# A sliding-window matmul: wider column groups, longer rows per load, fewer and larger weight loads

## The chip, the cores and the metric

The kernel runs on one core of a Trainium2 chip. The core has a matrix engine (TensorE, PE in the profile, with PEld for its weight loads), VectorE (DVE), ScalarE (ACT), GpSimd (POOL) and SyncE (SP). They share an on-chip memory (SBUF, 128 partitions), TensorE writes its sums to a second one (PSUM), and 16 DMA engines move data between SBUF and the external memory (HBM). A DMA is issued by an instruction on SP, ACT or POOL; of these only POOL's DMAs change the data type under way ("casting"). The metric is the device time in microseconds (us) of one execution. One MiB below is 1,048,576 bytes, and sizes of loads are given on their fp32 side, where they are read.

## The reference: what is computed

```python
B, S, D, W = 4, 4096, 4096, 64        # x (B,S,D), w (D,D) fp32, offsets (B,) int64
for b in range(B):
    o = int(offsets[b])
    results.append(x[b, o:o+W] @ w)
return np.stack(results)
```

Four windows of 64 rows, each at an offset known only at run time, are multiplied by the same 4096 x 4096 matrix w. Stacked, that is a 256 x 4096 matrix times w. The kernel reads 64 MiB of w and 4 MiB of x and writes 4 MiB.

## The kernel before

The windows are taken in two pairs (`G` = 2, index `g`); the two windows of a pair fill the 128 partitions of `xpair[g]`. The contraction over D runs in 32 k tiles of 128 rows of w. The output's columns are done in four groups `ng` of `NG` = 1024 columns, each in two halves of `NT` = 512 (index `j`).

Loads of w. The first three k tiles of group 0 come as plain fp32 DMAs from SP and ACT (L70) and are cast to fp16 by ACT (L79). Everything else of w comes as casting DMAs on POOL, one k tile of one group at a time: 128 rows of 1024 values, so 4 KB read per row and 0.5 MiB per load, into one of 36 buffers `wh`. Eight are issued at once (L74); the rest follow in the order of use (L112). The very last k tile of the last group is loaded in two halves (L107, `wlast`).

x. The offsets are loaded by SP to SBUF (L68), read into POOL registers (L83), and used as addresses by four casting DMAs on POOL (L94), each 64 rows of 4096 values, 16 KB read per row and 1 MiB per load. They stand in POOL's order behind the eight loads of L74 and ahead of those of L112.

Transposes. TensorE multiplies each 128 x 128 block of `xpair[g]` with an identity (L125), which leaves the transposed block in PSUM, and VectorE copies eight blocks at a time as fp16 into `xT[g]` (L132).

Main loop. For each group, for each k tile, for g and j, TensorE runs one matmul of 128 x 512 (L146). PSUM is four tiles of 1024 columns; odd and even groups use different pairs of them, so that one group's results can be copied out (ACT L159/L164, VectorE L160/L165) while the next group runs. Group 0 is stored by SP and ACT at once (L161, L162). Groups 1 and 2 are stored by POOL (L167). The last group is finished half by half (L175), copied out (L187, L188) and stored by SP and ACT (L192 to L196).

Order. Tile, the framework, places the waits between engines and schedules instructions; each engine then works through its own list in order. On POOL, every load of w stands ahead of the stores of L167. POOL's DMAs use eight completion semaphores in turn, so each DMA from the ninth on waits until the one eight places earlier has landed; a load also waits until its buffer's last reader is done.

Of the kernel before, what the change touches and what calls it, by code (L numbers as in the profile page):

```python
# [9 lines left out]
@with_exitstack  # L10
def kernel(
    ctx: ExitStack,
    tc: tile.TileContext,
    x: bass.AP,
    w: bass.AP,
    offsets: bass.AP,
    out: bass.AP,
):
    nc = tc.nc
    fp32 = mybir.dt.float32  # L20
    fp16 = mybir.dt.float16

    B, S, D = x.shape
    _, N = w.shape
    WIN = out.shape[1]
    P = 128
    KT = 128
    NT = 512
    NG = 1024
    n_k = D // KT  # L30
    n_ng = N // NG
    n_sub = NG // NT
    G = B // 2

    POOL = mybir.EngineType.Pool

    const_pool = ctx.enter_context(tc.tile_pool(name="const", bufs=1))
    x_pool = ctx.enter_context(tc.tile_pool(name="xp", bufs=1))
    wh_pool = ctx.enter_context(tc.tile_pool(name="wh", bufs=36))
    w32_pool = ctx.enter_context(tc.tile_pool(name="w32", bufs=1))  # L40
    whh_pool = ctx.enter_context(tc.tile_pool(name="whh", bufs=2))
    st_pool = ctx.enter_context(tc.tile_pool(name="st", bufs=1))
    sth_pool = ctx.enter_context(tc.tile_pool(name="sth", bufs=4))
    psum_pool = ctx.enter_context(tc.tile_pool(name="ps", bufs=1, space=bass.MemoryType.PSUM))

    identity = const_pool.tile([P, P], fp16, name="identity")
    off_t = const_pool.tile([1, B], mybir.dt.int64, name="off_t")

    xpair = [x_pool.tile([P, D], fp16, name=f"xpair{g}") for g in range(G)]
    xT = [x_pool.tile([P, D], fp16, name=f"xT{g}") for g in range(G)]  # L50

    ps = [psum_pool.tile([P, NG], fp32, name=f"ps{t}") for t in range(4)]

    wh_tiles = {}

    def w_tile(ng, ki):
        t = wh_pool.tile([P, NG], fp16, name="wh", tag="wh")
        wh_tiles[(ng, ki)] = t
        return t

    def w_src(ng, ki):
        return w[ki * KT : (ki + 1) * KT, ng * NG : (ng + 1) * NG]

    N_EARLY = 3
    early_q = [nc.sync, nc.scalar, nc.sync]
    w32 = [w32_pool.tile([P, NG], fp32, name=f"w32_{k}") for k in range(N_EARLY)]

    nc.sync.dma_start(out=off_t[:], in_=offsets[None, :])  # L68
    for k in range(N_EARLY):
        early_q[k].dma_start(out=w32[k][:], in_=w_src(0, k))  # L70

    n_pre = 8
    for ki in range(N_EARLY, N_EARLY + n_pre):
        nc.gpsimd.dma_start(out=w_tile(0, ki)[:], in_=w_src(0, ki))  # L74

    make_identity(nc, identity[:])

    for k in range(N_EARLY):
        nc.scalar.copy(out=w_tile(0, k)[:], in_=w32[k][:])  # L79

    off_i32 = off_t.bitcast(mybir.dt.int32)
    off_vals = [
        nc.values_load(  # L83
            off_i32[0:1, 2 * b : 2 * b + 1],
            engines=[POOL],
            min_val=0,
            max_val=S - WIN,
        )
        for b in range(B)
    ]  # L90

    for b in range(B):
        g, m = divmod(b, 2)
        nc.gpsimd.dma_start(  # L94
            out=xpair[g][m * WIN : (m + 1) * WIN, :],
            in_=x[b][bass.ds(off_vals[b], WIN), :],
        )

    wlast = [
        whh_pool.tile([P, NT], fp16, name="whl", tag="whl") for _ in range(n_sub)  # L100
    ]
    for ng in range(n_ng):
        for ki in range(N_EARLY + n_pre if ng == 0 else 0, n_k):
            if ng == n_ng - 1 and ki == n_k - 1:
                for j in range(n_sub):
                    cs = ng * NG + j * NT
                    nc.gpsimd.dma_start(  # L107
                        out=wlast[j][:],
                        in_=w[ki * KT : (ki + 1) * KT, cs : cs + NT],
                    )  # L110
            else:
                nc.gpsimd.dma_start(out=w_tile(ng, ki)[:], in_=w_src(ng, ki))  # L112

    stage = {}
    for ng in (1, 2):
        for g in range(G):
            stage[(ng, g)] = st_pool.tile(
                [P, NG], fp32, name=f"stage{ng}{g}", tag=f"stage{ng}{g}"
            )

    for g in range(G):
        for t in range(4):
            for q in range(8):
                k = 8 * t + q
                nc.tensor.matmul(  # L125
                    out=ps[t][:, q * KT : (q + 1) * KT],
                    lhsT=xpair[g][:, k * KT : (k + 1) * KT],
                    rhs=identity[:],
                    start=True,
                    stop=True,  # L130
                )
            nc.vector.tensor_copy(  # L132
                out=xT[g][:, t * NG : (t + 1) * NG], in_=ps[t][:]
            )

    for ng in range(n_ng):
        par = ng % 2
        acc = [ps[2 * par], ps[2 * par + 1]]
        last = ng == n_ng - 1
        cs = ng * NG  # L140
        n_full = n_k - 1 if last else n_k
        for ki in range(n_full):
            whk = wh_tiles[(ng, ki)]
            for g in range(G):
                for j in range(n_sub):
                    nc.tensor.matmul(  # L146
                        out=acc[g][:, j * NT : (j + 1) * NT],
                        lhsT=xT[g][:, ki * KT : (ki + 1) * KT],
                        rhs=whk[:, j * NT : (j + 1) * NT],
                        start=(ki == 0),  # L150
                        stop=(ki == n_k - 1),
                    )
        if not last:
            if ng == 0:
                st0 = [
                    st_pool.tile([P, NG], fp32, name=f"stage0{g}", tag="stage0")
                    for g in range(G)
                ]
                nc.scalar.copy(out=st0[0][:], in_=acc[0][:])  # L159
                nc.vector.tensor_copy(out=st0[1][:], in_=acc[1][:])  # L160
                nc.sync.dma_start(out=out[0:2, :, cs : cs + NG], in_=st0[0][:])  # L161
                nc.scalar.dma_start(out=out[2:4, :, cs : cs + NG], in_=st0[1][:])  # L162
            else:
                nc.scalar.copy(out=stage[(ng, 0)][:], in_=acc[0][:])  # L164
                nc.vector.tensor_copy(out=stage[(ng, 1)][:], in_=acc[1][:])  # L165
                for g in range(G):
                    nc.gpsimd.dma_start(  # L167
                        out=out[2 * g : 2 * g + 2, :, cs : cs + NG],
                        in_=stage[(ng, g)][:],
                    )  # L170
        else:
            ki = n_k - 1
            for j in range(n_sub):
                for g in range(G):
                    nc.tensor.matmul(  # L175
                        out=acc[g][:, j * NT : (j + 1) * NT],
                        lhsT=xT[g][:, ki * KT : (ki + 1) * KT],
                        rhs=wlast[j][:],
                        start=False,
                        stop=True,  # L180
                    )
                hs = cs + j * NT
                sth = [
                    sth_pool.tile([P, NT], fp32, name="sth", tag="sth")
                    for _ in range(G)
                ]
                nc.scalar.copy(out=sth[0][:], in_=acc[0][:, j * NT : (j + 1) * NT])  # L187
                nc.vector.tensor_copy(  # L188
                    out=sth[1][:], in_=acc[1][:, j * NT : (j + 1) * NT]
                )  # L190
                if j == 0:
                    nc.sync.dma_start(out=out[0:2, :, hs : hs + NT], in_=sth[0][:])  # L192
                    nc.sync.dma_start(out=out[2:4, :, hs : hs + NT], in_=sth[1][:])
                else:
                    nc.scalar.dma_start(out=out[0:2, :, hs : hs + NT], in_=sth[0][:])
                    nc.sync.dma_start(out=out[2:4, :, hs : hs + NT], in_=sth[1][:])  # L196


# [28 lines left out]
```

## Time and profile before

| what | value |
|---|---|
| median of 10 runs | 188.76 us (188.65 to 189.15) |
| profiled execution | 188.69 us |
| its span | 187.0 us |
| mean granted TensorE clock | 0.987 |
| PE busy | 132.0 us (71%) in 576 matmuls |
| VectorE, ScalarE, POOL busy | 14.3, 8.5, 71.9 us |
| HBM read, written | 71.30 MB, 4.19 MB: 404 GB/s over the span |
| POOL's DMA queue | 19040 packets, 36.97 MB |
| a load of w by L112, from issue to landing | 9.5 us (median) |
| first x load issued, last x load landed | 9.26 us, 28.38 us |
| first main matmul | 31.80 us |

The span runs from the first to the last record of the profiled execution; its own time is 1.7 us longer. "Busy" of a DMA engine is the time that packets took. GB/s and MB of the DMA rows count the bytes written, so a casting load shows half of what it reads. In the DMA packets of POOL's queue, each row of a load or store is one packet, and each DMA adds 16 small ones, which report that it is complete.

### The profile page before, as it was taken

To read this page: it belongs to the slowest core of one execution; us is meant where nothing else is said; L and a number is where in the kernel's file an instruction comes from. 1 tells how busy PE (TensorE), PEld (TensorE's weight loads), DVE (VectorE), ACT (ScalarE), POOL (GpSimd) and SP (SyncE) were. 2 spreads that over 40 slices of the span, in tenths; PEclk is the share of its full clock that TensorE was granted. 3 is DMA by queue.
4 is the path that set the end of the run, shared out by engine and by line. 5 is a ranking of instruction groups with operands and counts; after the bars stand their busy time and mean duration, and the time that the engine had idled before them with its cause. 6 is when DMAs were issued, how large, how long until landed. Compare 5 with 4: busy or idle time off the path is not lost.

```text
span 187.0 us, 1496 instructions
## 1 busy us (share of the span) xinstructions
PE 132.0 (71%) x576; PEld 56.0 (30%) x576; DVE 14.3 (8%) x13; ACT 8.5 (5%) x9; POOL 71.9 (38%) x140
## 2 busy tenths in 40 slices
PE   0000079999999967688788888888888888788820
PEld 0000078444444422223332332332323323323300
DVE  0000079200000020000002000000020000000020
ACT  2410000000002000000002000000020000000020
POOL 7343124333343433344344434434443426344200
PEclk9999999999999999999999999999999999999995
DMA  5999999999999999999999999999999999999994
GB/s 148 291 203 219 217 203 209 210 209 209 210 209 209 248 225 241 230 209 209 210 209 209 209 209 209 210 209 209 211 209 209 210 209 209 209 210 209 254 415 164
DMA packets 20344, 40.72 MB, mean 218 GB/s; under 512 B 2290, under 2 KB 2546, under 8 KB 20082
## 3 DMA queue, kind: packets, MB, share of 16 engines
q0 software_dynamic: 19040, 36.97, 102.3%
q1 hardware_dynamic: 866, 2.36, 3.3%
q10 hardware_dynamic: 432, 1.31, 2.2%
q8 instruction: 4, 0.07, 0.1%
q14 instruction: 2, 0.02, 0.0%
HBM read 71.30 MB, written 4.19 MB: 404 GB/s over the span
## 4 chain that ended last, share of the span: by engine, by line
DMA 70%; PE 18%; issue 5%; POOL 2%; DVE 0%; ACT 0%; POOLq 0%
DMA wh<-in_w_dram 63%; PE ps L146 15%; DMA xpair<-in_x_dram 8%; PE ps L125 2%; POOL wh L112 1%; POOL wh L74 1%; PE ps L175 1%; DVE sth L188 0%; ACT sth L187 0%; POOLq L112 0%; POOLq L211 0%
## 5 line engine op out<-in xcount | busy, mean ns | idle before, releaser
L146 PE MATMUL ps<-wh,xT 128*128 128x512 f16 x508 | 123.9, 378 | 22.4 <-DMA wh<-in_w_dram 22.3
L112 POOL DMA_DIRECT2D wh<-in_w_dram x116 | 61.5, 531 | 92.3 <-DMA wh<-in_w_dram 74.6
L146 PEld LDWEIGHTS <-xT 128*128 128x128 f16 x508 | 49.0, 97 | 96.8 <-issue 45.9
L125 PE MATMUL ps<-identity,xpair 128*128 128x128 f16 x64 | 7.1, 310 | 24.7 <-DMA xpair<-in_x_dram 24.7
L125 PEld LDWEIGHTS <-xpair 128*128 128x128 f16 x64 | 6.7, 144 | 24.9 <-issue 24.9
L132 DVE CAST xT<-ps 128x1024 f16<-128x1024 f32 x8 | 9.2, 1218 | 24.7 <-PE ps L125 24.7
L165 DVE COPY stage<-ps 128x1024 f32<-128x1024 f32 x2 | 2.5, 1225 | 68.0 <-PE ps L146 68.0
L164 ACT COPY stage<-ps 128x1024 f32<-128x1024 f32 x2 | 2.0, 1012 | 77.4 <-PE ps L146 77.4
L74 POOL DMA_DIRECT2D wh<-in_w_dram x8 | 4.4, 585 | 0.8 <-POOLq L211 0.8
L188 DVE COPY sth<-ps 128x512 f32<-128x512 f32 x2 | 1.4, 692 | 38.5 <-PE ps L175 38.5
L94 POOL DMA_DIRECT2D xpair<-in_x_dram x4 | 2.1, 522 | 5.5 <-DMA wh<-in_w_dram 5.5
L160 DVE COPY stage<-ps 128x1024 f32<-128x1024 f32 x1 | 1.2, 1225 | 34.7 <-DMA out_dram<-stage 34.7
L167 POOL DMA_DIRECT2D out_dram<-stage x4 | 2.1, 534 | 3.1 <-DMA wh<-in_w_dram 3.1
L159 ACT COPY stage<-ps 128x1024 f32<-128x1024 f32 x1 | 1.0, 1013 | 49.0 <-PE ps L146 49.0
L79 ACT CAST wh<-w 128x1024 f16<-128x1024 f32 x3 | 3.0, 1042 | 4.6 <-DMA w<-in_w_dram 4.6
L187 ACT COPY sth<-ps 128x512 f32<-128x512 f32 x2 | 1.2, 586 | 38.9 <-PE ps L175 38.9
L175 PE MATMUL ps<-whl,xT 128*128 128x512 f16 x4 | 1.3, 378 | 0.5 <-ACT sth L187 0.5
L107 POOL DMA_DIRECT2D whl<-in_w_dram x2 | 1.1, 530 | 1.3 <-DMA wh<-in_w_dram 1.3
L79 ACT ACT_TABLE_LOAD x1 | 1.3, 1283 | 1.3 <-PEq L211 1.3
L175 PEld LDWEIGHTS <-xT 128*128 128x128 f16 x4 | 0.4, 97 | 1.1 <-issue 0.5
masks.py:199 POOL TENSOR_SCALAR_AFFINE_SELECT identity<-identity 128x128 f16<-128x128 f16 x1 | 0.3, 289 | 0.1
masks.py:197 POOL MEMSET identity<- 128x128 f16 x1 | 0.3, 290 | 0.0
(4 smaller groups left out, 0.4 us busy)
## 6 DMA issues: line engine op xcount, KB each, us to landing
wh<-in_w_dram POOLq DMA_DIRECT2D x124, 256.0 KB, 9.5
xpair<-in_x_dram POOLq DMA_DIRECT2D x4, 512.0 KB, 12.8
out_dram<-stage POOLq DMA_DIRECT2D x4, 512.0 KB, 8.3
w<-in_w_dram SPq DMA_DIRECT2D x2, 512.0 KB, 6.3
out_dram<-sth SPq DMA_DIRECT2D x3, 256.0 KB, 5.6
w<-in_w_dram ACTq DMA_DIRECT2D x1, 512.0 KB, 4.3
out_dram<-stage SPq DMA_DIRECT2D x1, 512.0 KB, 8.3
out_dram<-stage ACTq DMA_DIRECT2D x1, 512.0 KB, 7.0
```

Source lines behind the costliest of these rows:

```text
L74: nc.gpsimd.dma_start(out=w_tile(0, ki)[:], in_=w_src(0, ki))
L79: nc.scalar.copy(out=w_tile(0, k)[:], in_=w32[k][:])
L94: nc.gpsimd.dma_start(out=xpair[g][m * WIN : (m + 1) * WIN, :], in_=x[b][bass.ds(off_vals[b], WIN), :],)
L112: nc.gpsimd.dma_start(out=w_tile(ng, ki)[:], in_=w_src(ng, ki))
L125: nc.tensor.matmul(out=ps[t][:, q * KT : (q + 1) * KT], lhsT=xpair[g][:, k * KT : (k + 1) * KT], rhs=identity[:], start=True, stop=True,)
L132: nc.vector.tensor_copy(out=xT[g][:, t * NG : (t + 1) * NG], in_=ps[t][:])
L146: nc.tensor.matmul(out=acc[g][:, j * NT : (j + 1) * NT], lhsT=xT[g][:, ki * KT : (ki + 1) * KT], rhs=whk[:, j * NT : (j + 1) * NT], start= ...
L164: nc.scalar.copy(out=stage[(ng, 0)][:], in_=acc[0][:])
L165: nc.vector.tensor_copy(out=stage[(ng, 1)][:], in_=acc[1][:])
L167: nc.gpsimd.dma_start(out=out[2 * g : 2 * g + 2, :, cs : cs + NG], in_=stage[(ng, g)][:],)
L175: nc.tensor.matmul(out=acc[g][:, j * NT : (j + 1) * NT], lhsT=xT[g][:, ki * KT : (ki + 1) * KT], rhs=wlast[j][:], start=False, stop=True,)
L188: nc.vector.tensor_copy(out=sth[1][:], in_=acc[1][:, j * NT : (j + 1) * NT])
```

## The change

The column groups become two of 2048 columns, with four matmul tiles of 512 in each; PSUM is eight tiles of one bank, and both groups use the same eight. The first k tile of w is loaded for all 4096 columns at once by one plain fp32 DMA on ACT (128 rows of 16 KB, 2 MiB) and cast by ACT in two pieces. On POOL one casting load of k tile 1 (128 rows of 8 KB, 1 MiB) comes first, then the identity, then the four x loads, whose offsets are read from SBUF to a register one by one, right ahead of each load, without the bounds checks at run time. All further loads of w read 8 KB rows; most of them take two k tiles in one DMA (2 MiB), and the last four or five of each group one. There are 12 buffers, each large enough for two k tiles. The eviction of the transposes is split between VectorE and ACT in pieces of 512 columns. The order of instructions is that of the program text (`manual_schedule`). The first group is stored by POOL after all loads, the second by ACT and SP, 1 MiB per DMA.

```diff
-    KT = 128
     NT = 512
-    NG = 1024
-    n_k = D // KT
+    NG = 2048
+    n_k = D // P
...
-    wh_pool = ctx.enter_context(tc.tile_pool(name="wh", bufs=36))
+    wh_pool = ctx.enter_context(tc.tile_pool(name="wh", bufs=12))
...
+    ps = [psum_pool.tile([P, NT], fp32, name=f"bank{t}") for t in range(8)]
...
+    ctx.enter_context(tc.manual_schedule())
 
     nc.sync.dma_start(out=off_t[:], in_=offsets[None, :])
-    for k in range(N_EARLY):
-        early_q[k].dma_start(out=w32[k][:], in_=w_src(0, k))
+    nc.scalar.dma_start(out=w0_32[:], in_=w[0:P, :])
+    off_i32 = off_t.bitcast(mybir.dt.int32)
 
-    n_pre = 8
-    for ki in range(N_EARLY, N_EARLY + n_pre):
-        nc.gpsimd.dma_start(out=w_tile(0, ki)[:], in_=w_src(0, ki))
+    def load(ng, ki, n):
+        t = wh_pool.tile([P, n * NG], fp16, name="wh", tag="wh")
+        nc.gpsimd.dma_start(
+            out=t[:].rearrange("p (t n) -> p t n", t=n),
+            in_=w[ki * P : (ki + n) * P, ng * NG : (ng + 1) * NG].rearrange(
+                "(t p) n -> p t n", p=P
+            ),
+        )
+        for i in range(n):
+            wh[(ng, ki + i)] = t[:, i * NG : (i + 1) * NG]
 
+    wh = {(ng, 0): w0_16[:, ng * NG : (ng + 1) * NG] for ng in range(n_ng)}
+    load(0, 1, 1)
     make_identity(nc, identity[:])
-    for k in range(N_EARLY):
-        nc.scalar.copy(out=w_tile(0, k)[:], in_=w32[k][:])
...
+    for b in range(B):
+        g, m = divmod(b, 2)
+        o = nc.values_load(
             off_i32[0:1, 2 * b : 2 * b + 1],
             engines=[POOL],
             min_val=0,
             max_val=S - WIN,
+            skip_runtime_bounds_check_because="offsets are drawn below S - WIN",
         )
+        nc.gpsimd.dma_start(
+            out=x16[g][m * WIN : (m + 1) * WIN, :],
+            in_=x[b][bass.ds(o, WIN), :]
+        )
+    for ng in range(n_ng):
+        for ki in range(n_k):
+            if (ng, ki) not in wh:
+                load(ng, ki, 2 if ki < n_k - 4 - (ki % 2) else 1)
...
+    nc.scalar.copy(out=w0_16[:, :NG], in_=w0_32[:, :NG])
+    nc.scalar.copy(out=w0_16[:, NG:], in_=w0_32[:, NG:])
...
+            dst = xT[g][:, t * NT : (t + 1) * NT]
+            if t % 2 == 0:
+                nc.vector.tensor_copy(out=dst, in_=ps[t][:])
+            else:
+                nc.scalar.copy(out=dst, in_=ps[t][:])
...
+        for ki in range(n_k):
             for g in range(G):
                 for j in range(n_sub):
+                    mm(g, j, ki, wh[(ng, ki)][:, j * NT : (j + 1) * NT], ki == 0, ki == n_k - 1)
+        for j in range(n_sub):
+            for g in range(G):
+                dst = stage[ng][g][:, j * NT : (j + 1) * NT]
+                if g == 0:
+                    nc.scalar.copy(out=dst, in_=ps[4 * g + j][:])
                 else:
+                    nc.vector.tensor_copy(out=dst, in_=ps[4 * g + j][:])
+        for g in range(G):
+            (q[g] if last else nc.gpsimd).dma_start(
+                out=out[2 * g : 2 * g + 2, :, ng * NG : (ng + 1) * NG],
+                in_=stage[ng][g][:],
+            )
```

More of the change, by code (lines that the diff above doesn't have):

```diff
@@ L38 @@
     x_pool = ctx.enter_context(tc.tile_pool(name="xp", bufs=1))
-    wh_pool = ctx.enter_context(tc.tile_pool(name="wh", bufs=36))
-    w32_pool = ctx.enter_context(tc.tile_pool(name="w32", bufs=1))
-    whh_pool = ctx.enter_context(tc.tile_pool(name="whh", bufs=2))
+    wh_pool = ctx.enter_context(tc.tile_pool(name="wh", bufs=12))
     st_pool = ctx.enter_context(tc.tile_pool(name="st", bufs=1))
-    sth_pool = ctx.enter_context(tc.tile_pool(name="sth", bufs=4))
     psum_pool = ctx.enter_context(tc.tile_pool(name="ps", bufs=1, space=bass.MemoryType.PSUM))
@@ L47 @@
     off_t = const_pool.tile([1, B], mybir.dt.int64, name="off_t")
-    xpair = [x_pool.tile([P, D], fp16, name=f"xpair{g}") for g in range(G)]
+    w0_32 = x_pool.tile([P, N], fp32, name="w0row")
+    w0_16 = x_pool.tile([P, N], fp16, name="w0half")
+    x16 = [x_pool.tile([P, D], fp16, name=f"xrow{g}") for g in range(G)]
     xT = [x_pool.tile([P, D], fp16, name=f"xT{g}") for g in range(G)]
[L52 to L66, printed above, removed]
-    nc.sync.dma_start(out=off_t[:], in_=offsets[None, :])
-    for k in range(N_EARLY):
-        early_q[k].dma_start(out=w32[k][:], in_=w_src(0, k))
-    n_pre = 8
-    for ki in range(N_EARLY, N_EARLY + n_pre):
-        nc.gpsimd.dma_start(out=w_tile(0, ki)[:], in_=w_src(0, ki))
-    make_identity(nc, identity[:])
-    for k in range(N_EARLY):
-        nc.scalar.copy(out=w_tile(0, k)[:], in_=w32[k][:])
-    off_i32 = off_t.bitcast(mybir.dt.int32)
-    off_vals = [
-        nc.values_load(
+    ps = [psum_pool.tile([P, NT], fp32, name=f"bank{t}") for t in range(8)]
+    ctx.enter_context(tc.manual_schedule())
+    nc.sync.dma_start(out=off_t[:], in_=offsets[None, :])
+    nc.scalar.dma_start(out=w0_32[:], in_=w[0:P, :])
[12 more added lines that the diff above has]
+    load(0, 1, 1)
+    make_identity(nc, identity[:])
+    for b in range(B):
+        g, m = divmod(b, 2)
+        o = nc.values_load(
             off_i32[0:1, 2 * b : 2 * b + 1],
@@ L87 @@
             max_val=S - WIN,
+            skip_runtime_bounds_check_because="offsets are drawn below S - WIN",
         )
[L89 to L93, printed above, removed]
         nc.gpsimd.dma_start(
-            out=xpair[g][m * WIN : (m + 1) * WIN, :],
-            in_=x[b][bass.ds(off_vals[b], WIN), :],
-        )
-    wlast = [
-        whh_pool.tile([P, NT], fp16, name="whl", tag="whl") for _ in range(n_sub)
-    ]
+            out=x16[g][m * WIN : (m + 1) * WIN, :],
+            in_=x[b][bass.ds(o, WIN), :]
+        )
     for ng in range(n_ng):
[L103 to L119, printed above, removed]
+        for ki in range(n_k):
[3 more added lines that the diff above has]
+    nc.scalar.copy(out=w0_16[:, NG:], in_=w0_32[:, NG:])
     for g in range(G):
-        for t in range(4):
-            for q in range(8):
-                k = 8 * t + q
+        for t in range(8):
+            for i in range(4):
+                k = 4 * t + i
                 nc.tensor.matmul(
-                    out=ps[t][:, q * KT : (q + 1) * KT],
-                    lhsT=xpair[g][:, k * KT : (k + 1) * KT],
+                    out=ps[t][:, i * P : (i + 1) * P],
+                    lhsT=x16[g][:, k * P : (k + 1) * P],
                     rhs=identity[:],
@@ L131, with mm @@
                 )
-            nc.vector.tensor_copy(
-                out=xT[g][:, t * NG : (t + 1) * NG], in_=ps[t][:]
-            )
+            dst = xT[g][:, t * NT : (t + 1) * NT]
[3 more added lines that the diff above has]
+                nc.scalar.copy(out=dst, in_=ps[t][:])
+    def mm(g, j, ki, rhs, start, stop):
+        nc.tensor.matmul(
+            out=ps[4 * g + j][:],
+            lhsT=xT[g][:, ki * P : (ki + 1) * P],
+            rhs=rhs,
+            start=start,
+            stop=stop,
+        )
@@ L136 @@
+    stage = [
+        [st_pool.tile([P, NG], fp32, name=f"stage{ng}{g}") for g in range(G)]
+        for ng in range(n_ng)
+    ]
+    q = [nc.scalar, nc.sync]
     for ng in range(n_ng):
-        par = ng % 2
-        acc = [ps[2 * par], ps[2 * par + 1]]
         last = ng == n_ng - 1
[L140 to L143, printed above, removed]
+        for ki in range(n_k):
             for g in range(G):
                 for j in range(n_sub):
[L146 to L193, printed above, removed]
-                else:
-                    nc.scalar.dma_start(out=out[0:2, :, hs : hs + NT], in_=sth[0][:])
-                    nc.sync.dma_start(out=out[2:4, :, hs : hs + NT], in_=sth[1][:])
```

## The prediction

> **What bounds the kernel now.** I read the page's row of busy tenths first, then the chain of work that ended last, then the stretches of time and the timeline.
>
> ```profile
> PE 132.0 (71%) x576; PEld 56.0 (30%) x576; DVE 14.3 (8%) x13; ACT 8.5 (5%) x9; POOL 71.9 (38%) x140
> ...
> DMA  5999999999999999999999999999999999999994
> ...
> DMA 70%; PE 18%; issue 5%; POOL 2%; DVE 0%; ACT 0%; POOLq 0%
> ```
>
> The DMA engines are full from the second slice to the last but one; TensorE is busy in 71% of the span, much of it latency. The group rows say the same from TensorE's side: its idle time ends on arriving weights (22.3 of 22.4 us).
>
> ```profile
> L146 PE MATMUL ps<-wh,xT 128*128 128x512 f16 x508 | 123.9, 378 | 22.4 <-DMA wh<-in_w_dram 22.3
> L112 POOL DMA_DIRECT2D wh<-in_w_dram x116 | 61.5, 531 | 92.3 <-DMA wh<-in_w_dram 74.6
> L187 ACT COPY sth<-ps 128x512 f32<-128x512 f32 x2 | 1.2, 586 | 38.9 <-PE ps L175 38.9
> L188 DVE COPY sth<-ps 128x512 f32<-128x512 f32 x2 | 1.4, 692 | 38.5 <-PE ps L175 38.5
> ```
>
> L112 waits 74.6 us for earlier weight loads: POOL's loads share eight completion semaphores, so a ninth load is issued when the first of eight has landed. The queue therefore always holds seven or eight loads, and the wait costs nothing. So the time is: start, bytes over rate, end. The chain, in order of time, gives the rate. Its columns are start, duration, what:
>
> ```profile
> 102.14 9.48 DMA wh<-in_w_dram
> ...
> 112.16 9.49 DMA wh<-in_w_dram
> ...
> 122.19 9.49 DMA wh<-in_w_dram
> ...
> 132.20 9.50 DMA wh<-in_w_dram
> ```
>
> Each step skips eight loads of 0.5 MiB (fp32 side): (132.20-102.14)/3 = 10.02 us for 4 MiB, 2.505 us per MiB, 418 GB/s read. The page's 209 GB/s counts the fp16 side. These loads have 4 KB source rows. The x loads have 16 KB rows, and the timeline shows their landings as the times at which POOL's next loads get released:
>
> ```profile
> 21.11 0.53 POOL L112 DMA_DIRECT2D wh<-in_w_dram  x1 [2.08 <-DMA xpair<-in_x_dram]
> ...
> 23.53 0.53 POOL L112 DMA_DIRECT2D wh<-in_w_dram  x1 [1.89 <-DMA xpair<-in_x_dram]
> ...
> 25.94 0.53 POOL L112 DMA_DIRECT2D wh<-in_w_dram  x1 [1.88 <-DMA xpair<-in_x_dram]
> 28.20 1.95 PEld L125 LDWEIGHTS <-xpair 128*128 128x128 f16 x19 [1.51 <-issue]
> 28.23 2.08 PE L125 MATMUL ps<-identity,xpair 128*128 128x128 f16 x18 [1.27 <-DMA xpair<-in_x_dram]
> 28.38 0.53 POOL L112 DMA_DIRECT2D wh<-in_w_dram  x1 [1.91 <-DMA xpair<-in_x_dram]
> ```
>
> (28.38-21.11)/3 = 2.423 us per MiB, 433 GB/s. Same queue, same cast, longer rows: 3.4% faster. This pair of numbers carries the forecast. The tail is read from stretches of 1 us (DMA share and GB/s are the last columns, the granted clock the one before):
>
> ```profile
> 176.00:177.00 1.00, 0.81 (x4) 0.29 (x3) 0.00 (x0) 0.00 (x0) 0.00 (x0) 1.00 1.16 307
> 178.00:179.00 1.00, 0.54 (x3) 0.19 (x2) 0.68 (x1) 0.59 (x1) 0.00 (x0) 1.00 1.04 426
> 182.00:183.00 1.00, 0.00 (x0) 0.00 (x0) 0.00 (x0) 0.00 (x0) 0.00 (x0) 0.60 1.05 408
> 184.00:185.00 1.00, 0.00 (x0) 0.00 (x0) 0.00 (x0) 0.00 (x0) 0.00 (x0) 0.50 0.34 129
> ```
>
> Casting loads show about 209, plain stores about 415, so at 307 the loads gave way at about 176.5. From there only stores run: the four of L167, queued on POOL behind every load, and the last four. 3 MiB until about 184.3; the span ends 2.7 us later. The stretches from 178 to 183 (426, 418, 422, 395, 408) average 414 GB/s, 2.53 us per MiB.
>
> The span therefore adds up so: first bytes at 2.0 (the stretch from 2 has share 0.77, the one before 0.14); 15.0 for 1.5 MiB fp32 and 4 MiB of the first casting loads (the eighth lands at 18.5 and its bytes are in about 1.5 earlier; at full rate 13.8, so 1.2 is ramp); 9.9 for x; 149.6 for the other 58.5 MiB of w and 1 MiB of stores; 7.8 for the last stores; 2.7 end: 187.0.
>
> **The change, part by part.** Bytes do not change: w 64 MiB and x 4 MiB read, 4 MiB written. Only rate, order and gaps can pay.
>
> *Row length.* 124 loads with 4 KB rows and two with 2 KB become 36 loads with 8 KB rows (1+13+4 in the first group, 13+5 in the second), 62 MiB in all. Per MiB a DMA engine takes 16 rows at 4 KB and 4 at 16 KB; the difference of 0.082 us over 12 rows is 6.8 ns per row, fewer completion packets included. At 8 KB it takes 8 rows: 2.423+4x0.0068 = 2.450 us per MiB (428 GB/s). This is interpolated, an estimate; its ends are 2.505 (row length gives nothing) and 2.423 (as x). 62.5x2.505 = 156.6 becomes 62x2.450 = 151.9: **-4.7 us** (between -1.3 and -6.4). Here the Trainium skill, "DMA: Bandwidth & Descriptors", section Bandwidth, gives two limits: about 358 GB/s on the HBM side for HBM to SBUF, and 435 for the SBUF ports. By the first, nothing can speed up at all and -1.3 would be the value; but the trace reads at 418 and 433 with this one core active, so I take the second, which says that x's rate is nearly all there is: 435 is 2.41 us per MiB, and 16 KB rows could not do much better.
>
> *Two k tiles in one load.* 13+13 of the loads (52 MiB) read two row blocks that lie 2 MiB apart. The same page, section Latency and other measured facts, speaks against such strides: copies whose partition rows are 2 MiB apart ran at 164 instead of some 214 GB/s. Applied in full to 52 MiB: 127.4 us/0.77 = 166, +38 us. The nearest row of this trace is L112 itself, whose consecutive loads lie 2 MiB apart too, but hardly overlap in one engine. In the changed kernel neighbouring partitions stay 16 KB apart and only a partition's second half is 2 MiB away, so I take 0 here, and keep the penalty as a rival. The other cost is granularity: TensorE gets 16 matmuls per 4.9 us. In the catching-up phase the chain has 126 in 27.38 us, 0.217 each: 16 take 3.5 us, so a 1.4 us pause per pair. The tail above has the granted clock fall in the stretch from 182, over 2.5 us after the last matmul (about 179.4), so 1.4 us should not lower it. If it did, 16 matmuls would take some 6.9 us and TensorE would bind, about 2 us per pair.
>
> *Buffers.* 36 of 0.5 MiB become 12 of up to 2 MiB. Eight loads outstanding, one or two in use by TensorE: 10 of 12. L112 now waits 6.4 us for TensorE ("PE ps L146", 10 times) without the DMA row dipping; a load that waits for a buffer still leaves seven in the queue. 0 us; if all cover were gone, the pause would be one pair's compute, 3.5 us.
>
> *First k tile.* 1.5 MiB plain on SP and ACT become 2 MiB in one plain load with 16 KB rows on ACT: 3.8 to 2x2.47 = 4.9: **+1.1** (the 0.5 MiB is taken out of the casting term). ACT's casts, two of 2048 columns at about 1.95 us each (1042 ns for 1024, 586 for 512), come before its share of the transposes' evictions, but w0 lands by about 12 and x's first half at about 16.
>
> *x early, offsets.* POOL now issues one load (about 0.55 us from 1.4), the identity, and then waits for the offsets; behind that wait stand the four x loads and every other w load. SP sends the offsets at 0.87 ahead of all else; I expect them near 3. Then 0.3 to 0.5 us per register load (the four now take 291 to 488 ns) plus 0.52 per x load: x issued by 8. The 3 MiB already queued last till about 9.5, so the DMA is not idle. If the offsets came after about 8, each microsecond later would cost one. x's 4 MiB keep their 9.9. TensorE's start moves from 23.4 to about 16 and its main loop from 31.8 to about 25; worth nothing, since bytes set the end. The eight 1024-column casts become 16 of 512 on two engines, 0.6 to 0.7 us each against 0.45 us of transposes per bank (3.57/32x4), alternating: hidden. At the group boundary TensorE waits about 1 us for banks, hidden by its slack (1.4 us in 4.9).
>
> *Stores and tail.* Stores with 8 KB rows save 8 rows per MiB for all but a quarter: 10.1 to 9.9, **-0.2**. Behind the last load POOL has 2 MiB of the first group's output: 2x2.475 = 4.95 us of cover, against about 5 us of POOL's stores now. Under it: the last tile lands about 1.7 after its bytes (176.5 to TensorE's release at 178.19), ACT's first copy starts 0.42 later, four copies take 2.4, and the plain store's first bytes come about 1.1 after issue (0.88 to 2.0 at the start): 5.6. **+0.65 us** of empty queue. The other half, on VectorE and SP, is ready at 1.7+1.4+2.8+1.1 = 7.0, when the first still has till 8.1 to run. Bounds: 0 to 2 us.
>
> Start ramp (1.2) and end (2.7) stay. Sum: -4.7+1.1-0.2+0.65 = **-3.15**. The profiled execution is 188.69 us with span 187.0; span about 183.85, time 185.54. The median is 188.76, 0.07 above: 185.6.
>
> **The rivals.** (a) Two row blocks 2 MiB apart slow the HBM reads: slower than before. Place: the 26 paired loads. The balance is gone once they lose 3.15/52 = 0.06 us per MiB (2.51 instead of 2.45, 418 GB/s); at 5% lost it is 185.6+6.4 = 192, at the page's ratio 224. For: the two halves run together in one load. Against: pitch between partitions unchanged. (b) Row length does nothing; x's 433 has another cause, since each x load is one contiguous MiB: -1.3+1.1+0+0.65 = +0.45, 189.2. Against: plain stores with 4 KB rows run at 414, close to w's 418, as a cost per row would have it. (c) 8 KB rows run at x's rate: 62x0.027 = 1.7 better, 183.9; with no gap in the tail 183.3. (d) TensorE becomes the bound through the clock: against it stands the pause of 1.4 us; about 185.6+26x2 = 238.
>
> **How the numbers follow.** The sum as worked out 0.70 (own range 184.4 to 187.0: 2.44 to 2.47 us per MiB, tail 0 to 1.5), (c) 0.09, (b) 0.10, (a) 0.09, (d) 0.02. Predicted 185.6. The range takes in (c) and (b)'s lower half, 183.7 to 189.0, and leaves out (a), (d) and the rest of (b). No change within 0.2% (0.38 us, about what this measurement can tell) is half of (b) and a little of the sum's upper end: 0.07. Slower: the other half of (b), (a), (d): 0.16. Faster 0.77.
>
> **What would show it.** In the middle the steady GB/s should read about 214 instead of 209, and pairs land 4.9 us apart. x's issues stand before 8 us with no dip in the DMA row's first slices. The granted clock stays near 1.0 in the middle. After the last load the stores' stretch shows one dip of under 1 us and lasts about 10.5 us. Wrong if: the steady rate is 209 or less, the clock shows halves, the DMA row has a hole by the offsets, or the tail's gap is over 2 us.

## The result and the profile after

The changed kernel takes 183.58 us (median of 8 runs, 183.34 to 183.60), the kernel before in the same comparison 188.83 us (28 runs). The ratio is 0.9718, with a 95% interval from 0.9709 to 0.9726: 2.8% faster. The forecast was 185.6 us with a range from 183.7 to 189.0. The direction was right; the gain of 5.25 us is 2.1 us more than the 3.15 forecast, and the time lies 0.1 us below the range.

The page of the changed kernel: busy time, the row of DMA shares, the chain, and two groups.

```profile
PE 123.0 (68%) x576; PEld 56.6 (31%) x576; DVE 10.5 (6%) x16; ACT 13.8 (8%) x19; POOL 27.6 (15%) x48
...
DMA  5999999999999999999999999999999999999995
...
DMA 89%; issue 3%; POOL 1%; DVE 1%; POOLq 1%; PE 1%; DVEq 0%
...
L108 PE MATMUL bank<-wh,xT 128*128 128x512 f16 x496 | 112.0, 379 | 32.4 <-DMA wh<-in_w_dram 32.3
...
L58 POOL DMA_DIRECT2D wh<-in_w_dram x36 | 23.8, 661 | 117.0 <-DMA wh<-in_w_dram 106.0
```

The DMA engines are still what binds: their row is full, and the chain now names DMA for 89% of the span. TensorE waits longer than before (32.4 us instead of 22.4); the experiments below show that this costs nothing. The profiled execution took 183.77 us with a span of 182.1.

The timeline of POOL in the middle of the changed kernel follows; each issue stands at the landing of the load eight places earlier.

```profile
46.70 0.70 POOL L58 DMA_DIRECT2D wh<-in_w_dram  x1 [4.27 <-DMA wh<-in_w_dram]
...
66.27 0.53 POOL L58 DMA_DIRECT2D wh<-in_w_dram  x1 [4.44 <-DMA wh<-in_w_dram]
...
85.85 0.69 POOL L58 DMA_DIRECT2D wh<-in_w_dram  x1 [4.27 <-DMA wh<-in_w_dram]
```

From 46.70 to 85.85 eight loads of 2 MiB land: 39.15/16 = 2.447 us per MiB, where the forecast had 2.450. The middle's rate is what was forecast, so the 2 us that the forecast lacks must lie at the ends. Compared with its sum: TensorE gets the last load of w at 171.43 (the sum's terms make 172.1), and from there to the end of the span it takes 10.7 us (sum 11.7).

### The profile page after: what moved, and what is told of

Its sections match the earlier page's. It is cut to its first block, busy times and chain, and to the rows that moved or that the text cites. A ratio compares the mean times of both kernels' runs of the same rounds, so it can differ in the third digit from the quotient of the medians.

```text
span 182.1 us, 1329 instructions
## 1 busy us (share of the span) xinstructions
PE 123.0 (68%) x576; PEld 56.6 (31%) x576; DVE 10.5 (6%) x16; ACT 13.8 (8%) x19; POOL 27.6 (15%) x48
## 3 DMA queue, kind: packets, MB, share of 16 engines
q10 hardware_dynamic: 288, 3.15, 4.6%
## 4 chain that ended last, share of the span: by engine, by line
DMA 89%; issue 3%; POOL 1%; DVE 1%; POOLq 1%; PE 1%; DVEq 0%
DMA wh<-in_w_dram 89%; DVE stage L133 1%; POOL wh L58 1%; PE bank L108 1%; POOLq L72 1%; POOL xrow L79 0%; DVEq L164 0%; POOL identity masks.py:197 0%; POOLq L79 0%; POOLq L58 0%; POOLq masks.py:199 0%; POOLq L153 0%
## 5 line engine op out<-in xcount | busy, mean ns | idle before, releaser
L108 PE MATMUL bank<-wh,xT 128*128 128x512 f16 x496 | 112.0, 379 | 32.4 <-DMA wh<-in_w_dram 32.3
L58 POOL DMA_DIRECT2D wh<-in_w_dram x36 | 23.8, 661 | 117.0 <-DMA wh<-in_w_dram 106.0
L94 PE MATMUL bank<-identity,xrow 128*128 128x128 f16 x64 | 7.1, 310 | 17.7 <-DMA xrow<-in_x_dram 17.7
L131 ACT COPY stage<-bank 128x512 f32<-128x512 f32 x8 | 4.1, 600 | 144.3 <-PE bank L108 144.3
L133 DVE COPY stage<-bank 128x512 f32<-128x512 f32 x8 | 5.0, 684 | 145.1 <-PE bank L108 145.1
L94 PEld LDWEIGHTS <-xrow 128*128 128x128 f16 x64 | 6.7, 144 | 17.9 <-issue 17.9
L103 DVE CAST xT<-bank 128x512 f16<-128x512 f32 x8 | 5.5, 692 | 19.6 <-PE bank L94 19.6
L105 ACT CAST xT<-bank 128x512 f16<-128x512 f32 x8 | 4.7, 585 | 7.1 <-PE bank L94 7.1
L108 PE MATMUL bank<-w0half,xT 128*128 128x512 f16 x16 | 4.4, 397 | 0.2 <-DVE stage L133 0.2
L88 ACT CAST w0half<-w0row 128x2048 f16<-128x2048 f32 x1 | 1.9, 1897 | 7.4 <-DMA w0row<-in_w_dram 7.4
L89 ACT CAST w0half<-w0row 128x2048 f16<-128x2048 f32 x1 | 1.9, 1892 | 0.0
```

The lines of the kernel that those rows point to most:

```text
L58: nc.gpsimd.dma_start(out=t[:].rearrange("p (t n) -> p t n", t=n), in_=w[ki * P : (ki + n) * P, ng * NG : (ng + 1) * NG].rearrange("(t p) ...
L88: nc.scalar.copy(out=w0_16[:, :NG], in_=w0_32[:, :NG])
L89: nc.scalar.copy(out=w0_16[:, NG:], in_=w0_32[:, NG:])
L94: nc.tensor.matmul(out=ps[t][:, i * P : (i + 1) * P], lhsT=x16[g][:, k * P : (k + 1) * P], rhs=identity[:], start=True, stop=True,)
L103: nc.vector.tensor_copy(out=dst, in_=ps[t][:])
L105: nc.scalar.copy(out=dst, in_=ps[t][:])
```

## The experiments

Times are medians of the timed runs, with the kernel before timed beside them (188.79 to 188.95). They are compared with the changed kernel's 183.58.

### What the middle's rate is made of

Four runs part the length of a row from the size of a load. The first cuts the changed kernel's loads by columns, which halves the rows and doubles the number of loads:

```diff
-        nc.gpsimd.dma_start(out=t[...], in_=w[ki * P : (ki + n) * P, ng * NG : (ng + 1) * NG]...)
+        for h in range(2):
+            c = ng * NG + h * H          # H = NG // 2
+            nc.gpsimd.dma_start(out=t[...][:, :, h * H : (h + 1) * H],
+                                in_=w[ki * P : (ki + n) * P, c : c + H]...)
```

> The changed kernel with each weight load cut into two by columns, so that rows are 4 KB again (72 loads instead of 36); nothing else moves. Row length sets the rate: 62 MiB x (2.505 - 2.447 us per MiB) = 3.6 us slower than the changed kernel, about 187.2 us, and the steady stretch shows 209 GB/s. If it is instead the smaller number of loads that pays (126 before, 36 after, here 72), about 40% of the gain is given back: near 185.6 us, steady stretch 212.

186.48 us (ratio to the kernel before 0.987, interval 0.985 to 0.989): 2.9 us are given back, between the two expectations.

The second cuts them by k tiles and keeps the rows:

```diff
-    wh_pool = ctx.enter_context(tc.tile_pool(name="wh", bufs=12))
+    wh_pool = ctx.enter_context(tc.tile_pool(name="wh", bufs=24))
-                load(ng, ki, 2 if ki < n_k - 4 - (ki % 2) else 1)
+                load(ng, ki, 1)
```

> The changed kernel with one k tile per load everywhere (62 loads of 1 MiB with 8 KB rows, 24 buffers of half the size). Row length sets the rate: within 0.3 us of the changed kernel, 183.5 to 183.9. If two row blocks 2 MiB apart in one load cost something, it is faster: below 183.2. If fewer loads pay, it is slower by 26/90 of the gain, about 185.1.

184.05 us (184.0 to 184.1), 0.47 us slower. So two row blocks 2 MiB apart in one load cost nothing that shows; rival (a) falls. But row length alone would have left the time within 0.3 us, and fewer loads alone would have moved it three times as far.

The third changes the kernel before, and only the number of k tiles per load (with buffers to match):

```diff
-                nc.gpsimd.dma_start(out=w_tile(ng, ki)[:], in_=w_src(ng, ki))
+                load(ng, ki, 2 if ki + 2 <= n_k - (ng == n_ng - 1) else 1)
```

> The kernel before with two k tiles per load (1 MiB, still 4 KB rows; buffers of twice the size). Row length sets the rate: no change beyond 0.3 us, 188.4 to 188.9. If fewer and larger loads pay: about half of the gain, 186 us.

187.25 us (ratio 0.991, 0.990 to 0.993): 1.6 us faster with the same 4 KB rows. "Row length sets the rate" is refuted as the whole cause; the size of a load counts too.

The fourth measures both costs by themselves, in one execution. It leaves out x, the transposes and the matmuls, and stores zeros; it only loads parts of w, 24 MiB for each of six shapes:

```diff
+    stretch("a", 4096, 1, 24)      # values per row, k tiles per load, MiB
+    stretch("b", 2048, 2, 24)
+    stretch("c", 2048, 1, 24)
+    stretch("d", 1024, 4, 24)
+    stretch("e", 1024, 1, 24)
+    stretch("f", 512, 4, 24)
```

> Loads of w alone, on the one POOL queue, 24 MiB for each of six shapes in turn: rows of 16 KB (2 MiB per load), 8 KB (two k tiles, 2 MiB), 8 KB (one k tile, 1 MiB), 4 KB (four k tiles, 2 MiB), 4 KB (one k tile, 0.5 MiB), 2 KB (four k tiles, 1 MiB). No x, no matmul; the stores hold zeros. A cost of 6.8 ns per row says 2.42, 2.45, 2.45, 2.50, 2.51 and 2.61 us per MiB. If the size of a load is what counts, the fourth is near the second (2.45) and the third and fifth stand apart from their partners.

The timeline of POOL in this kernel, at the landings that part the stretches (a line's start is the landing of the load eight places earlier). The first half of a stands beside the stores, so it is read from the landing of its sixth load on; one issue in f comes late, at 342.99, for no reason that the profile shows, so f is read from its first eleven loads, ahead of it:

```profile
44.57 0.72 POOL L37 DMA_DIRECT2D wh<-in_w_dram  x1 [4.12 <-DMA wh<-in_w_dram]
...
73.77 0.71 POOL L37 DMA_DIRECT2D wh<-in_w_dram  x1 [4.16 <-DMA wh<-in_w_dram]
...
132.52 0.53 POOL L37 DMA_DIRECT2D wh<-in_w_dram  x1 [4.37 <-DMA wh<-in_w_dram]
...
191.50 0.74 POOL L37 DMA_DIRECT2D wh<-in_w_dram  x1 [1.72 <-DMA wh<-in_w_dram]
...
250.92 0.53 POOL L37 DMA_DIRECT2D wh<-in_w_dram  x1 [4.42 <-DMA wh<-in_w_dram]
...
311.07 0.74 POOL L37 DMA_DIRECT2D wh<-in_w_dram  x1 [0.52 <-DMA wh<-in_w_dram]
...
339.02 0.74 POOL L37 DMA_DIRECT2D wh<-in_w_dram  x1 [1.79 <-DMA wh<-in_w_dram]
```

| stretch | row | per load | us over MiB | us per MiB | 2.409 + 0.0036 x rows + 0.020 x loads |
|---|---|---|---|---|---|
| a | 16 KB | 2 MiB | 29.20 / 12 | 2.433 | 2.433 |
| b | 8 KB | 2 MiB | 58.75 / 24 | 2.448 | 2.448 |
| c | 8 KB | 1 MiB | 58.98 / 24 | 2.458 | 2.458 |
| d | 4 KB | 2 MiB | 59.42 / 24 | 2.476 | 2.477 |
| e | 4 KB | 0.5 MiB | 60.15 / 24 | 2.506 | 2.507 |
| f | 2 KB | 1 MiB | 27.95 / 11 | 2.541 | 2.544 |

"Rows" are those that one DMA engine takes per MiB (4, 8, 16, 32), "loads" the loads per MiB. Two pairs with equal rows (b and c, d and e) give 19 and 20 ns per load; a to b and b to d give 3.7 and 3.5 ns per row. The three constants are fitted to these six values, so the small residuals alone prove little; the full kernels below are the test. What is left, 2.409 us per MiB, is 435 GB/s. That number is the limit of the SBUF ports in the Trainium skill ("DMA: Bandwidth & Descriptors", Where 436 GB/s comes from); the 358 GB/s of the HBM side is passed by every row of the table, with this one core active. But 435 is what is read. The cast halves it, and what these loads write to the SBUF is about 218 GB/s, so the equal number does not show that the ports set the rate. The forecast drew its upper limit for x's rate from there; no run here tells what sets it.

The forecast's 6.8 ns per row was therefore 3.6 ns and a hidden load cost: a 4 KB-row load carried 0.5 MiB and an x load 1 MiB. The interpolation came out right for 8 KB because the change halves the rows and, with larger loads, cuts that second cost as well. In the full kernels the two costs come near: rows4k 62 MiB x 8 x 3.6 ns + 36 x 20 ns = 2.5 us (measured 2.9), onek 26 x 20 ns = 0.5 (0.47), before_pairs 61 x 20 ns = 1.2 (1.6; there the last x load also lands at 28.08 instead of 28.38).

### The early x

```diff
     load(0, 1, 1)
     make_identity(nc, identity[:])
+    load(0, 2, 2)
+    load(0, 4, 2)
     for b in range(B):
```

> The changed kernel with the x loads behind two more loads of two k tiles (4 MiB), so that x lands about 9.8 us later, near 31. If bytes, rows and loads set the end, TensorE's later start is hidden: 183.4 to 183.8, as the changed kernel. If the early x is where the extra 2 us of gain come from, some of them go: above 184.3.

183.51 us (183.47 to 183.56): no difference. TensorE's earlier start is worth nothing in time, as forecast.

### The two ends

The start, cut as before:

```diff
-    nc.scalar.dma_start(out=w0_32[:], in_=w[0:P, :])
+    for i in range(4):
+        c = slice(i * 1024, (i + 1) * 1024)
+        (nc.scalar, nc.sync)[i % 2].dma_start(out=w0_32[:, c], in_=w[0:P, c])
...
-    load(0, 1, 1)
+    for h in range(2):                   # k tile 1 in two halves of 1024 columns
+        nc.gpsimd.dma_start(out=t[:, c], in_=w[P : 2 * P, c])
```

> The changed kernel with the start cut as before: the first k tile's row in four plain loads of 0.5 MiB with 4 KB rows on ACT and SP in turn, and k tile 1 in two loads of 0.5 MiB. By the costs of the sweep (3.6 ns per row, 20 ns per load) it is 0.2 us slower than the changed kernel, 183.8. If the start's ramp was shortened by the single large load (x was complete 0.5 to 0.7 us earlier than the sum has it), it is 0.7 us slower: 184.2 to 184.4.

184.65 us (184.49 to 184.89): 1.07 us slower, more than either expectation, and far more than rows and loads cost (0.2, an estimate from the sweep). The stretches of 1 us from the start, first the changed kernel's, then this one's (granted clock, DMA share and GB/s are the last columns):

```profile
1.00:2.00 1.00, 0.00 (x0) 0.00 (x0) 0.00 (x0) 0.72 (x1) 0.62 (x1) 1.00 0.43 98
2.00:3.00 1.00, 0.00 (x0) 0.00 (x0) 0.00 (x0) 0.56 (x1) 0.55 (x3) 1.00 1.15 229
3.00:4.00 1.00, 0.00 (x0) 0.00 (x0) 0.00 (x0) 0.00 (x0) 0.47 (x1) 1.00 0.50 197
4.00:5.00 1.00, 0.00 (x0) 0.00 (x0) 0.00 (x0) 0.00 (x0) 0.59 (x2) 1.00 1.15 492
```

```profile
1.00:2.00 1.00, 0.00 (x0) 0.00 (x0) 0.00 (x0) 0.00 (x0) 0.62 (x1) 1.00 0.08 16
2.00:3.00 1.00, 0.00 (x0) 0.00 (x0) 0.00 (x0) 0.00 (x0) 0.93 (x4) 1.00 0.87 229
3.00:4.00 1.00, 0.00 (x0) 0.00 (x0) 0.00 (x0) 0.00 (x0) 0.18 (x1) 1.00 0.78 209
4.00:5.00 1.00, 0.00 (x0) 0.00 (x0) 0.00 (x0) 0.00 (x0) 0.54 (x2) 1.00 0.85 340
```

Up to 5 us the changed kernel has 98+229+197+492 = 1016 KB written, this one 794, much as the kernel before, with 29, 197, 229 and 369. These sums overstate the lead. The profile counts a packet whole in the stretch in which it starts, and the first packets are 16 KB long in the changed kernel and 4 KB here. With each packet's bytes spread over the time that it took, and the fp32 side of casting loads counted, the traces give a lead of about 75 KB read at 5 us and 245 KB at 10 us, which is 0.6 us at 428 GB/s; the first packets start at 1.9 us in both. At 10 us the kernel before stands where this one does, within 5 KB. So the loads do not begin earlier; they run faster in the first 10 us.

The last x load lands at 22.19 instead of 21.41. This 0.78 us is all of what parts the two profiled executions (184.49 and 183.77 us); their medians are 1.07 apart. The start, whose ramp the sum had left at its 1.2 us, is shortened by the changed first loads. Two things differ at once here, the plain row and k tile 1, and with them x's first load is issued 0.5 us later (4.05 instead of 3.54). Which of them counts is not told apart.

The stores at the end:

```diff
+                if last:                 # behind each copy of 512 columns
+                    c = slice(j * NT, (j + 1) * NT)
+                    q[g].dma_start(out=out[2 * g : 2 * g + 2, :, ng * NG + c.start : ng * NG + c.stop],
+                                   in_=stage[ng][g][:, c])
...
-        for g in range(G):
-            (q[g] if last else nc.gpsimd).dma_start(...)
+        if not last:
+            for g in range(G):
+                nc.gpsimd.dma_start(...)
```

> The changed kernel with the last group's two stores of 1 MiB cut into eight of 256 KB with 2 KB rows, each issued behind its copy, as the kernel before ended. Rows and loads cost 2 MiB x 24 rows x 3.6 ns + 6 x 20 ns = 0.3 us more; the gap of about 0.45 us in the stores goes. Sum: 183.4. If the small stores are what made the end of the kernel before longer (2.8 us from the end of the bytes to the end of the span, 2.2 in the changed one), 0.6 us comes on top: 184.0.

184.37 us (184.18 to 184.55), 0.8 us slower. The gap did close: in stretches of 0.5 us the changed kernel has 328 and 311 GB/s from 174.0 to 175.0, this one 414 and 336; with each packet spread over its own time, the shares of the DMA engines are 0.92 and 0.63 there, and 1.01 and 1.04 here. What follows cost more. The last stretches, the changed kernel's first:

```profile
179.50:180.00 0.50, 0.00 (x0) 0.00 (x0) 0.00 (x0) 0.00 (x0) 0.00 (x0) 0.50 0.63 262
180.00:180.50 0.50, 0.00 (x0) 0.00 (x0) 0.00 (x0) 0.00 (x0) 0.00 (x0) 0.50 0.12 49
180.50:181.00 0.50, 0.00 (x0) 0.00 (x0) 0.00 (x0) 0.00 (x0) 0.00 (x0) 0.50 0.04 16
181.00:182.10 1.10, 0.00 (x0) 0.00 (x0) 0.00 (x0) 0.00 (x0) 0.00 (x0) 0.50 0.00 0
```

```profile
179.50:180.00 0.50, 0.00 (x0) 0.00 (x0) 0.00 (x0) 0.00 (x0) 0.00 (x0) 0.50 0.57 217
180.00:180.50 0.50, 0.00 (x0) 0.00 (x0) 0.00 (x0) 0.00 (x0) 0.00 (x0) 0.50 0.21 82
180.50:181.00 0.50, 0.00 (x0) 0.00 (x0) 0.00 (x0) 0.00 (x0) 0.00 (x0) 0.50 0.14 53
181.00:182.90 1.90, 0.00 (x0) 0.00 (x0) 0.00 (x0) 0.00 (x0) 0.00 (x0) 0.50 0.01 2
```

Most bytes are out at the same time, but with small stores they thin out more slowly: 82, 53 and still some GB/s after 180, where the changed kernel has 49, 16 and none. At the end of both kernels SP waits for every DMA's semaphore, one semaphore after the other. Its waits from the landing of the last store on, again the changed kernel's first (number of instructions, then ns of one as least, median and most, then first and last start; the last two of each belong to a final meeting of all engines):

```profile
L164 SPq EVENT_SEMAPHORE  x3: 17/17/28, 181.2 to 182.1; - x3
```

```profile
L171 SPq EVENT_SEMAPHORE  x10: 17/28/28, 181.5 to 182.8; - x10
```

This splits the 0.75 us between the two spans (182.1 and 182.9). The last store lands 0.3 us later, though the gap is gone. The other 0.45 us stands behind it: 1.36 us to the end of the span instead of 0.91. Two stores use two semaphores, and the store that lands last is on the later one. Eight stores use eight, the one that lands last is on the first that SP comes to, and SP has seven more waits to go through, 0.06 us apart.

The kernel before ends in the same way, though with four stores of 256 KB behind four of 0.5 MiB: its last store lands 1.29 us ahead of the end. That small stores cause the 0.8 us is shown, and these two traces put over half of it into SP's closing waits; why the bytes thin out more slowly is not shown.

Four stores of half the size, by the same edit behind every second copy:

> The changed kernel with the last group's stores cut into four of 0.5 MiB with 4 KB rows, each behind two copies. Rows and loads cost 2 x 8 x 3.6 ns + 2 x 20 ns = 0.1 us; the gap of 0.45 us goes: 183.2. If the queue is not empty there, or the end grows with the number of stores, no faster than the changed kernel: 183.6 or more.

183.65 us (183.57 to 183.66): no faster. Its bytes thin out about 0.25 us sooner (344 and 123 GB/s where the changed kernel has 377 and 262, from 179.0 to 180.0), but 66 and 8 GB/s trail until about 181. The last store lands at 181.07 instead of 181.22. It is on the last of its four semaphores, and 0.92 us follow it, as with two stores. The span is 182.0 against 182.1, so closing the gap brings nothing that the medians show.

### Do the parts add up?

> The changed kernel with both ends as before, and the rows and loads of the middle as changed: the start in small loads (0.5 MiB, 4 KB rows) and the last group in eight stores of 256 KB. If start and end are separate costs, each measured alone (1.07 and 0.79 us), they add: 183.58 + 1.86 = 185.4, which is about the forecast of 185.6. If they are one cost seen twice, about 184.7.

185.42 us (185.24 to 185.74; ratio 0.982, 0.980 to 0.984). The edit is both cuts above at once. The two ends add: 183.58 + 1.07 + 0.79 = 185.44.

The last of this row also takes the middle back to one k tile and 4 KB rows per load, with 24 buffers:

```diff
-                load(ng, ki, 2 if ki < n_k - 4 - (ki % 2) else 1)
+                load(ng, ki, 1)          # and each load in two halves of 1024 columns
```

> The same, and the middle in loads of one k tile with 4 KB rows as well (0.5 MiB each, 124 loads in all with the start's two). Column groups of 2048, the early x and the order of the text stay. Rows 62 x 8 x 3.6 ns = 1.8 and 86 loads x 20 ns = 1.7 on top of 185.4: 188.9, as the kernel before. If the wider groups, the early x or the new order gain or lose anything of their own, the difference to the kernel before shows it.

188.95 us; ratio to the kernel before 1.0003, interval 0.9994 to 1.0013. With DMA shapes like those of before at the start, in the middle and at the end (not the same ones: it ends with 2 MiB in stores of 256 KB, the kernel before with 1 MiB), the new kernel is as slow as the old one. Column groups of 2048, the early x, the register loads without checks, the split evictions and the order of the text are together worth nothing in time that shows, beyond making the larger DMAs possible. Single ones may still cancel; only the early x was tried alone.

### Further in the same direction

```diff
-    wh_pool = ctx.enter_context(tc.tile_pool(name="wh", bufs=12))
+    wh_pool = ctx.enter_context(tc.tile_pool(name="wh", bufs=6))
-                load(ng, ki, 2 if ki < n_k - 4 - (ki % 2) else 1)
+                load(ng, ki, 4 if ki < n_k - 7 else 2 if ki < n_k - 4 - (ki % 2) else 1)
```

> The changed kernel with four k tiles per load (4 MiB, 8 KB rows) where two were taken, six buffers of twice the size: 24 loads of w instead of 36. At 20 ns per load it is 0.24 us faster, 183.3. If six buffers are too few (one in use, at most five loads in the queue, and the single loads at the groups' ends take whole buffers), the queue runs dry at the group boundary and it is slower, by up to the 2 us that TensorE takes for its last tile there.

183.45 us (183.28 to 184.19; ratio 0.972, 0.970 to 0.974). The difference of 0.13 to the changed kernel is within the spread, so no gain is claimed. The queue does not run dry (its steady stretches show 213 to 216 GB/s), but TensorE's pauses grow. Its timeline in the first group and at the start of the second, and the granted clock in the second, in stretches of 1 us:

```profile
51.03 8.75 PE L108 MATMUL bank<-wh,xT 128*128 128x512 f16 x32 [2.65 <-DMA wh<-in_w_dram]
...
70.65 7.07 PE L108 MATMUL bank<-wh,xT 128*128 128x512 f16 x32 [2.78 <-DMA wh<-in_w_dram]
...
104.84 9.38 PE L108 MATMUL bank<-wh,xT 128*128 128x512 f16 x32 [4.72 <-DMA wh<-in_w_dram]
114.69 7.07 PE L108 MATMUL bank<-wh,xT 128*128 128x512 f16 x32 [0.47 <-DMA wh<-in_w_dram]
```

```profile
108.00:109.00 1.00, 1.00 (x3) 0.29 (x2) 0.00 (x0) 0.00 (x0) 0.00 (x0) 0.50 1.03 213
109.00:110.00 1.00, 1.00 (x5) 0.42 (x4) 0.00 (x0) 0.00 (x0) 0.00 (x0) 0.73 1.11 221
110.00:111.00 1.00, 1.00 (x6) 0.44 (x5) 0.00 (x0) 0.00 (x0) 0.00 (x0) 1.00 1.05 213
```

After a pause of 4.72 us the clock is at 0.50, and 32 matmuls take 9.38 us instead of 7.07. Pauses of about 2.7 us do it at some places and not at others: 8.75 us after 2.65, 7.07 after 2.78. TensorE just keeps pace with 9.8 us per load of 4 MiB, which leaves still larger loads little room.

> The same with the first of the last group's two stores cut into two of 0.5 MiB, both on SP, and the second store on ACT. If the gap in the stores (0.25 to 0.45 us) can be closed without the longer end that more stores bring, 0.2 us faster than with four k tiles per load alone, 183.1; if the third store lengthens the end as four and eight did, no difference.

The edit, on top of the four k tiles, gives the first of the last group's stores in two halves to SP and the second store whole to ACT.

183.48 us (183.39 to 183.51): no difference, as with four stores.

## Why the prediction was right and wrong

The runs that put the ends and then the middle back split the gain in three. Beside them stand the forecast's terms. In these, the 0.5 MiB that moved from the casting loads to the plain row (1.25 us) is taken from the middle's gain and set against the start's cost:

| part | forecast | measured | from |
|---|---|---|---|
| middle: rows and loads of 62 MiB | -3.4 | -3.5 | undo_all to ends_old |
| start: plain row, ramp | -0.15 | -1.1 | start_old |
| end: stores, gap, last packets | +0.45 | -0.8 | stores256 |
| sum | -3.1 | -5.4 | |

The measured parts make 0.1 us more than the gain of 5.25, since undo_all is that much slower than the kernel before.

*Row length* (-4.7 with the moved half MiB): right in size, wrong in what it is made of. The step "6.8 ns per row, fewer completion packets included" mixed two costs of about equal weight here, 62 x 8 x 3.6 ns = 1.8 us from the rows and about 90 loads x 20 ns = 1.8 us from the number of loads. It also rested on three landing intervals of x, 2.423 us per MiB; the four including the first (18.50 to 28.38) give 2.47, and the sweep's costs give 2.443 for such a load. That it landed within 0.1 us owes something to luck. (In its sum over the span, 58.5 MiB of w and 1 MiB of stores stand at 149.6 us; at its own rates they make 149.1. The change takes nothing from this.)

*Two k tiles, buffers, early x, offsets, evictions* at 0: right. The pauses of TensorE left the granted clock at 1.00 in every stretch of 10 us read from 40 to 160. The last x load was issued at 6.35. The rivals (a) and (d) did not occur. Nor did (b): rows do cost, though about half of the middle's gain came from the number of loads. (c), 183.9, was near in time but for another reason: the 8 KB rows did not run at x's rate.

*"Start ramp (1.2) and end (2.7) stay"*: this step failed. Both were read off the kernel before and carried over as constants, while the change alters what stands in them. The changed first loads took 1.1 us off (0.8 in the traces, when x is complete), against 0.15 in the sum; why is open beyond the 0.2 for rows and loads. At the end, two stores of 1 MiB in place of small ones left 2.2 us from the end of the bytes (counted as if they had run at full rate to their end) to the end of the span, in place of 2.8. Of this 0.6 us, about 0.4 is SP's closing waits: 0.91 us from the landing of the last store, in place of 1.29.

*The gap in the stores*: the mechanism was there and over-sized. The sum had 0.65 us; the dip from 174.0 to 175.0 (328 and 311 of about 418 GB/s) lost about 0.25, and the packets' own times give the same. Closing it by smaller stores brought no time.

The range was too narrow for one reason: its lower end held only the uncertainty of the rate and the gap, and nothing for start and end, which were taken as known.

## What to carry to other kernels

In a kernel that its DMA engines bind, count the cost of bytes, rows and loads as separate terms, and get each from shapes that differ in one of them only; two shapes that differ in both can't tell them apart. What stands before the first full stretch and after the last one is not a constant: first loads and last stores that are large and few shortened both here, by as much together as half of the middle's gain. At the end, look also at what follows the last landing. And in short stretches, remember that a packet counts where it starts. Work that such a kernel hides (an earlier start of TensorE, split evictions) brings no time, and pauses of TensorE have to stay short: loads of 2 MiB left the clock alone, loads of 4 MiB did not.

## What the runs showed of the hardware

- Casting loads of w on one queue, with the queue kept full, took 2.409 us per MiB, 3.6 ns per row on each DMA engine and 20 ns per load: a fit within 0.003 us per MiB for six shapes from 2 to 16 KB rows and from 0.5 to 2 MiB per load.
- Two row blocks 2 MiB apart in one load showed no penalty: 2.448 us per MiB against 2.458 with one block per load. The penalty that the forecast weighed does not show in this pattern, in which partitions stay 16 KB apart.
- Eight last stores of 256 KB instead of two of 1 MiB made the kernel 0.8 us longer: the last one landed 0.3 us later, and SP's closing waits behind it took 0.45 us more, 0.06 us for each of seven.
- The granted clock was at 0.50 after a pause of TensorE of 4.7 us, and 32 matmuls took 9.38 us instead of 7.07. It stayed at 1.00 over pauses of up to 1.4 us; pauses of about 2.7 us gave both.
